# Splitting paged key loads 11 : 5 instead of 8 : 8 between SyncE's queue and GpSimd's indirect loads

## The chip, the cores and the metric

The kernel runs on one core of one Trainium2 chip. The metric is device time in microseconds (us) for one execution of the whole program, the median of several runs. Engines are named as the profile names them: PE is TensorE's matmul side and PEld its weight loads, DVE is VectorE, ACT is ScalarE, POOL is GpSimd, SP is SyncE, which here does nothing but issue transfers. An engine's queue that issues a DMA is written SPq or ACTq.

## The reference

The program is one inference step of two decoder layers on a prompt of 1024 tokens and on a sample group of 8 sequences with 4 new tokens each (32 rows), all in float32. Layer 0 mixes tokens by multi-scale pooling and retention, layer 1 by multi-head latent attention; each layer ends in a gated MLP with a width-3 causal convolution. Only layer 1's sample attention is touched by the change. Each of the 8 sequences has 8192 past tokens in a paged cache, 64 pages of 128 tokens, found through a page table:

```
ckv_past = cache_ckv[layer_idx, page_table].reshape(B, P, KV_LORA)      # 8 x 8192 x 256
kpe_past = cache_kpe[layer_idx, page_table].reshape(B, P, QK_ROPE)      # 8 x 8192 x 64
q_lat  = einsum('bqhd,chd->bqhc', q_nope, w_uk)
s_past = einsum('bqhc,bkc->bhqk', q_lat, ckv_past) + einsum('bqhr,bkr->bhqk', q_pe, kpe_past)
p      = softmax(concat([s_past, s_new]) * MLA_SCALE, masked)
o_lat  = einsum('bhqk,bkc->bqhc', p[..., :P], ckv_past) + einsum('bhqk,bkc->bqhc', p[..., P:], c_kv)
```

The prompt's attention of the same layer (8 heads, causal, 1024 x 1024) needs nothing from the cache.

## The kernel before, in words

**Stages.** The program runs layer 0 (mixer, output projection, MLP), then layer 1's projections, then `attention()`, then the output projection `om` and layer 1's MLP. Weights come in units of 128 x 1024 numbers on SP's queue and are split into a high and a low part, because each product is made of three fast matmuls.

**attention().** It holds two streams of work for PE. The prompt stream is `heads()` (keys and values of a head), `scores()` and `outs()`. The sample stream is `keys()`, `turn()`, `soft()` and `values()`. The past is read twice: as key pages, feature-major, 128 rows of 320 numbers (160 KB a page), and as value blocks of four pages, token-major, 128 rows of 4 x 257 numbers (526,336 bytes, by the shape of `vt`).

- `load_keys()` (line 1548) goes over 8 sequences, and for each over 8 key tiles `kt` of 8 pages. A tile comes from a ring of `KRAW = 4`. Line 1561 decides for each page of the tile who loads it. With `j % 4 < KSP` and `KSP = 2`, pages 0, 1, 4 and 5 go to SP and pages 2, 3, 6 and 7 to GpSimd: 256 pages each in the whole stage.
- An SP page is `page_load()` (line 1908): a `value_load` reads the page's row number from the table in SBUF into a register of SP, and a plain DMA reads 128 rows from there. The `value_load` may be issued once the DMA eight SP pages before it has been issued.
- A GpSimd page is one indirect DMA: GpSimd itself makes the list of rows from the table.
- `load_values()` (line 1569) takes a tile `vt` from a ring of `VRAW = 5` and loads each of 128 value blocks (16 for each sequence) by an indirect DMA of GpSimd. Key and value loads of GpSimd stand in one queue, in the order in which the planner came to them.
- `keys()` (line 1580) takes two key tiles at once, which is called a pair below: 16 pages. It gives 16 + 4 narrow matmuls for each pair (line 632) and gives both tiles back. There are 32 pairs.
- `values()` (line 1660) takes two `vt` tiles at once and gives 16 narrow matmuls, on the average for four `vt` tiles per pair of key tiles.

**What sets the order.** All these are generators. `Pipe.run()` picks the next step for PE when the program is written: the first in priority that is ready by a set of modelled clocks (`Clocks`, line 294 on). The instructions are then issued in that order, and each engine works through its own list in order; nothing is reordered on the chip by what really arrives. A clock stands for each of PE, DVE, ACT, POOL and SP, and one more list for the transfers:

```
issue = {"sp": 480.0, "act": 50.0, "pool": 1040.0}[eng]
...
end = self.transfer(t + issue + 700.0, size / RATE)
```

These are lines 354 and 357: a DMA takes so many ns of its issuing engine, and then `size / RATE` ns of one path, on which transfers go one after the other (`RATE = 310` bytes per ns, which is GB/s). `Engine.__getattr__` (line 398) adds 590 ns to SP's clock for each `value_load`. The sample stream has priority 5.0 and the prompt stream 5.5 to 6.0, as long as the sample stream has spent no more than `SHARE = 1.2` times the PE time of the prompt stream; so the planner gives PE sample work when its modelled data is there, and prompt work in between. The same clocks plan all other stages too, where each weight unit is one DMA of SP.

After the key pages SP's list holds the loads `uvn` and `prm`, and then the weights of `om`.

Of the kernel before, what the change touches and what calls it, by code (L numbers as in the profile page):

```python
# [43 lines left out]
CHUNKS = [(0, CH), (CH, CH), (2 * CH, CH)]  # L44
ENDS = [(0, 352), (352, 288), (640, 256), (896, 160)]
NEG = -1.0e30
KSP = 2
KRAW = 4
VRAW = 5
NST = 5  # L50
# [13 lines left out]
END2 = (2, 3)  # L64
AHEAD = 0.0
PRICE = 0.42
RATE = 310.0
SHARE = 1.2
DVEX = 0.0
HEADS = [("uqn", 0), ("uqn", 1), ("uqp", 0), ("uqp", 1), ("uqn", 2), ("uqn", 3)]  # L70
# [223 lines left out]
class Clocks:  # L294
# [52 lines left out]
    def count(self, eng, op, ins, outs):  # L347

        ext = [a for a in list(ins) + list(outs) if len(a.shape) > 1]
        n = max(int(np.prod(a.shape[1:])) for a in ext) if ext else 1  # L350
        psum = any(a.space == PSUM for a in list(ins) + list(outs))
        if "dma" in op:
            size = int(np.prod(outs[0].shape)) * 4.0
            issue = {"sp": 480.0, "act": 50.0, "pool": 1040.0}[eng]
            t = max([self.at[eng]] + [self.ready(a, eng) for a in ins] + [self.free(a) for a in outs])
            self.at[eng] = t + issue
            end = self.transfer(t + issue + 700.0, size / RATE)
            for a in outs:
                self.write(a, end, "dma")
            for a in list(ins) + list(outs):  # L360
                self.used[a.name] = max(self.used.get(a.name, 0.0), end)
            if outs[0].space != DRAM:
                self.last = max(self.last, end + self.SEEN["dma"])
            return
        small = sum(len(a.shape) == 2 and a.shape[1] == 1 for a in list(ins[1:]) + list(outs))
        if eng == "act":
            cost = n / 1.2 + (51.0 if psum else 94.0) + (93.0 if small and n > 1 else 0.0)
        elif eng == "dve":
            fast = op in ("tensor_copy", "tensor_scalar") and not psum
            cost = (66.0 + (6.0 * n if op == "reciprocal" else n / 2 if fast else n)) / 0.96  # L370
            if n > 1 and op in ("tensor_scalar", "scalar_tensor_tensor"):
                cost += 63.0 * small
        else:
            cost = {"tensor_tensor": 150.0 + 2.1 * n, "memset": 37.0 + 0.9 * n}.get(op, 120.0 + 3.3 * n)
        self.issue(eng, cost, ins, outs)
# [16 lines left out]
class Engine:  # L392
# [5 lines left out]
    def __getattr__(self, op):  # L398
        f = getattr(self._real, op)
        if op == "value_load":  # L400
            self._clocks.at["sp"] += 590.0
            return f

        def call(*args, **kw):
            r = f(*args, **kw)  # L405
            aps = [a for a in args if isinstance(a, bass.AP)]
            ins = aps[1:] + [a for k, a in kw.items() if k != "accum_out" and isinstance(a, bass.AP)]
            outs = aps[:1] + [a for k, a in kw.items() if k == "accum_out" and isinstance(a, bass.AP)]
            self._clocks.count(self._name, op, ins, outs)
            return r  # L410

        return call
# [149 lines left out]
class Kernel:  # L562
# [906 lines left out]
    def attention(self):  # L1469
# [35 lines left out]
        def load_queries():  # L1505

            for e in range(2):
                nc.sync.dma_start(qraw[64 * e:64 * e + 64], self.qpd[:, :, SEQ:])
            for e in range(2):
                nc.sync.dma_start(qpe0[64 * e:64 * e + 64], self.qpd[:, 0, :SEQ])  # L1510
            for e in range(2):
                s = slice(64 * e, 64 * e + 64)
                nc.vector.tensor_copy(qpS[s, :, e].rearrange("p b h i -> p h b i"), qraw[s].rearrange("p h (b i) -> p h b i", b=NB))
            pipe.give("p")
            pipe.fire("qps")
# [32 lines left out]
        def load_keys():  # L1548
            for b in range(NB):
                kix, o = (kix1, (b - 1) * NPG) if b else (self.kix0, 0)  # L1550
                if b == 0:
                    load_queries()
                    nc.sync.dma_start(kix1, io["ptb"][:, NPG:])
                    yield ("rd", kix1)
                    self.rows(kix1, 128.0, "part", ap.tile([128, 512], F32, tag="sev", name="rows", bufs=NEV)[:, :NB * NPG - NPG])
                for u in range(NPG // 8):
                    yield ("res", "kt", 1)
                    kt = ap.tile([128, 8, 320], F32, tag="kt", name="kt", bufs=KRAW)
                    for j in range(8):
                        n = o + u * 8 + j  # L1560
                        if j % 4 < KSP:
                            kdma.append(self.page_load(kdma, kt[:, j], kix[0:1, n:n + 1]))
                        else:
                            nc.gpsimd.indirect_dma_start(kt[:, j], None, io["kT"],
                                                         bass.IndirectOffsetOnAxis(ap=kix[:, n:n + 1], axis=0))
                    raws[b, u] = kt
                    pipe.fire(("kraw", b, u))
# [327 lines left out]
        pipe.late = XRA  # L1895
        pipe.add(prepare(), 1)
        pipe.add(load_keys(), -3)
        pipe.add(load_values(), -3)
        pipe.add(values(), sprio)
# [115 lines left out]
```

## Time and profile before

| what | value |
|---|---|
| median of 3 runs | 2901.79 us (2899.61 to 2902.35) |
| profiled execution, its own time | 2902.8 us |
| span of the profiled instructions | 2901.0 us |
| granted PE clock over the span | 0.97 |
| PE busy | 2743.6 us, 95% of the span |
| POOL busy | 850.1 us, 29% |
| DMA | 301.78 MB, mean 104 GB/s |
| key pages by SP, by GpSimd | 256, 256 |
| value blocks by GpSimd | 128 |

The page gives busy time of each engine over the whole span. The share of POOL, 29%, is an average over stages: in the second part of the page, 40 slices of 72.5 us each with the busy share in tenths, POOL stands at 7 in six slices in the middle and at 0 to 4 elsewhere. Windows are given in us from the start of the span; the stage `attention()` lies at about 1409 to 1967. In a view of windows the columns are the length, then for each engine its busy time with the number of its instructions, then PE's granted clock, the share of time in which the 16 DMA engines were busy, and the rate that they moved. In a view of waits each row says who waited for whom, with the sum in us, the number of times and the longest. A wait "<- issue" is time between two instructions in which the engine waited for nothing that the profile shows.

### The profile page before, as it was taken

What the parts mean: (1) busy time and instruction counts of PE and PEld (TensorE: products, weight loads), DVE (VectorE), ACT (ScalarE), POOL (GpSimd) and SP (SyncE); (2) the same over time, 40 slices, a digit from 0 to 9 for tenths busy, and PEclk for the clock granted to TensorE, in tenths of its full rate; (3) what the DMA queues carried; (4) which work ended last, traced back from release to release, by engine and by line L of the source; (5) the groups of instructions that cost most, each with busy time, mean ns of one, the idle gap of its engine ahead of it and who ended that gap; (6) DMA issues with size and microseconds to landing.
All of it is one profiled execution on the core that took longest, in us unless ns stands there. A gap on an engine that the chain in (4) does not pass through costs nothing.

```text
span 2901.0 us, 43639 instructions
## 1 busy us (share of the span) xinstructions
PE 2743.6 (95%) x16897; PEld 2459.3 (85%) x16897; DVE 1417.1 (49%) x2721; ACT 867.5 (30%) x1831; POOL 850.1 (29%) x884
## 2 busy tenths in 40 slices
PE   8999998999999999989888989799899999999997
PEld 6777997999999999879745555469789999999996
DVE  4444547544444444774343535355764444444455
ACT  3323435211211222243233433243431211211223
POOL 1222334010110010333577777643410110011112
PEclk9999999999999999999999999899999999999997
DMA  3111420211111111132888999874211111111101
GB/s 137 60 56 50 118 80 23 65 44 37 59 44 38 58 44 52 38 100 67 254 293 280 310 318 314 274 236 140 66 44 37 59 44 33 63 45 46 49 25 60
DMA packets 127055, 301.78 MB, mean 104 GB/s; under 512 B 20960, under 2 KB 71952, under 8 KB 126720
## 3 DMA queue, kind: packets, MB, share of 16 engines
q1 hardware_dynamic: 75648, 159.62, 16.9%
q0 software_dynamic: 32576, 113.73, 11.5%
q10 hardware_dynamic: 18624, 25.63, 3.0%
q8 instruction: 134, 2.20, 0.3%
q14 instruction: 73, 0.60, 0.1%
HBM read 283.71 MB, written 15.21 MB: 103 GB/s over the span
## 4 chain that ended last, share of the span: by engine, by line
PE 77%; DMA 6%; DVE 5%; issue 5%; POOL 4%; ACT 2%; SPq 0%; POOLq 0%; DVEq 0%; ACTq 0%
PE bank L616 70%; PE bank L632 3%; DMA kt<-in_kT,kix 3%; DMA vt<-in_vrow,vix 2%; PE sc L616 2%; POOL kt L405 2%; PE bank L638 1%; DVE x L405 1%; DVE ln_v L405 1%; DVE z L405 1%; POOL z L405 1%; DMA p<-qpd 1%; DVE wl L405 1%; DMA kt<-in_kT 1%; POOL vt L405 0%
## 5 line engine op out<-in xcount | busy, mean ns | idle before, releaser
L616 PE MATMUL bank<-x,wh 128*128 128x352 f32 x5664 | 1379.7, 326 | 18.1 <-DVE x L405 16.6
L616 PEld LDWEIGHTS bank<-x,wh 128*128 128x128 f32 x5664 | 992.8, 190 | 32.7 <-DVE x L405 21.7
L616 PE MATMUL bank<-x,wl 128*128 128x352 f32 x2832 | 915.7, 324 | 9.4 <-DVE wl L405 9.4
L616 PEld LDWEIGHTS bank<-x,wl 128*128 128x128 f32 x2832 | 537.1, 190 | 11.1 <-DVE wl L405 10.6
L405 ACT CAST wh<-wr 128x1024 fp32r<-128x1024 f32 (+1 forms) x196 | 202.7, 1041 | 669.9 <-PE bank L616 638.6
L405 DVE SCALAR_TENSOR_TENSOR z<-z,bank 128x352 f32<-128x352 f32 (+3 forms) x440 | 219.6, 511 | 325.6 <-PE bank L616 319.6
L616 PE MATMUL bank<-ah,wh 128*128 128x352 f32 (+3 forms) x1088 | 352.8, 324 | 0.0
L616 PE MATMUL bank<-ah,wl 128*128 128x352 f32 (+3 forms) x1088 | 350.3, 322 | 0.0
L616 PE MATMUL bank<-al,wh 128*128 128x352 f32 (+3 forms) x1088 | 350.2, 322 | 0.0
L405 POOL TENSOR_TENSOR wl<-wr,wh 128x1024 fp32r<-128x1024 f32 (+1 forms) x60 | 145.3, 2430 | 638.3 <-PE bank L616 391.6
L405 POOL DMA_INDIRECT kt<-in_kT,kix x256 | 252.1, 985 | 84.3 <-issue 59.9
L405 DVE TENSOR_TENSOR wl<-wr,wh 128x1024 fp32r<-128x1024 f32 (+1 forms) x138 | 176.9, 1284 | 147.9 <-ACT wh L405 143.3
L616 PE MATMUL bank<-wh,x 128*128 128x512 f32 (+3 forms) x720 | 238.7, 393 | 8.1 <-ACT wh L405 8.1
L616 PEld LDWEIGHTS bank<-ah,wh 128*128 128x128 f32 x1088 | 207.6, 191 | 1.3 <-issue 0.2
L616 PEld LDWEIGHTS bank<-al,wh 128*128 128x128 f32 x1088 | 207.4, 191 | 1.4 <-issue 0.2
L616 PEld LDWEIGHTS bank<-ah,wl 128*128 128x128 f32 x1088 | 207.5, 191 | 0.6 <-DVE wl L405 0.6
L405 POOL COPY co<-a 128x2 f32<-128x2 f32 x44 | 39.2, 892 | 553.9 <-ACT a L405 553.9
L405 DVE SCALAR_TENSOR_TENSOR y<-a,prm,y 128x352 f32<-128x352 f32 (+1 forms) x264 | 166.1, 629 | 9.8
L405 DVE TENSOR_TENSOR g<-y,bank 128x352 f32<-128x352 f32 (+2 forms) x176 | 71.5, 427 | 202.2 <-PE bank L616 201.1
L405 DVE TENSOR_SCALAR y<-a,prm 128x352 f32<-128x352 f32 x132 | 77.0, 583 | 183.6 <-ACT a L405 178.1
L616 PEld LDWEIGHTS bank<-wh,x 128*128 128x128 f32 (+1 forms) x720 | 127.6, 181 | 32.5 <-ACT wh L405 8.1
L405 POOL DMA_INDIRECT vt<-in_vrow,vix x128 | 125.8, 983 | 72.8 <-PE bank L632 28.1
(234 smaller groups left out, 3184.4 us busy)
## 6 DMA issues: line engine op xcount, KB each, us to landing
wr<-in_w_up SPq DMA_DIRECT2D x88, 512.0 KB
kt<-in_kT SPq DMA_DIRECT2D x256, 160.0 KB
wr<-in_w_dn SPq DMA_DIRECT2D x44, 512.0 KB
wr<-in_w_h SPq DMA_DIRECT2D x16, 512.0 KB
wr<-in_w_oe SPq DMA_DIRECT2D x16, 512.0 KB
wr<-in_w_om SPq DMA_DIRECT2D x16, 512.0 KB
z<-in_xT SPq DMA_DIRECT2D x12, 352.0 KB
z<-in_xT ACTq DMA_DIRECT2D x3, 1408.0 KB
```

What stands on the lines that cost most here:

```text
L405: r = f(*args, **kw)
L616: self.nc.tensor.matmul(out, lhsT, rhs, start=start, stop=stop)
L632: self.nc.tensor.matmul(out[32 * g:32 * g + m], lhsT, rhs, start=start, stop=stop, tile_position=(0, 32 * g))
L638: self.nc.tensor.transpose(out, in_, self.ident[:in_.shape[0], :in_.shape[0]])
```

## The change

It does three things.

1. `KSP` becomes 11 and the rule on line 1561 counts pages over two tiles: page number `n16 = u * 8 + j` goes to SP when `n16 * 11 % 16 < 11`. Of each 16 pages, 0, 2, 3, 5, 6, 8, 9, 11, 12, 14 and 15 go to SP, five in the first tile of a pair and six in the second; 1, 4, 7, 10 and 13 go to GpSimd. In all SP loads 352 pages and GpSimd 160.
2. The clocks' prices: a DMA takes 530 ns of SP instead of 480 and 1250 ns of GpSimd instead of 1040, and a `value_load` 570 ns instead of 590.
3. The clocks' path: `RATE` 380 instead of 310. This and the prices enter the planner alone; they change no instruction, but the order in which instructions of each engine are issued.

```
-KSP = 2
+KSP = 11
...
-RATE = 310.0
+RATE = 380.0
...
-            issue = {"sp": 480.0, "act": 50.0, "pool": 1040.0}[eng]
+            issue = {"sp": 530.0, "act": 50.0, "pool": 1250.0}[eng]
...
-            self._clocks.at["sp"] += 590.0
+            self._clocks.at["sp"] += 570.0
...
-                        if j % 4 < KSP:
+                        if (u * 8 + j) * KSP % 16 < KSP:
                             kdma.append(self.page_load(kdma, kt[:, j], kix[0:1, n:n + 1]))
                         else:
                             nc.gpsimd.indirect_dma_start(kt[:, j], None, io["kT"],
```

## The prediction

> **What bounds the kernel now.** First the page's slices, to find the stage; in each row a digit is the busy share of a slice in tenths.
>
> ```profile
> PE   8999998999999999989888989799899999999997
> POOL 1222334010110010333577777643410110011112
> DMA  3111420211111111132888999874211111111101
> ```
>
> POOL and DMA are high only in slices 20 to 26. The view of windows, cut at that stage's borders, measures it:
>
> ```profile
> core 0: us, PE busy (x) PEld busy (x) DVE busy (x) ACT busy (x) POOL busy (x), PEclk, DMA share, GB/s
> 0.00:1409.00 1409.00, 1357.63 (x7990) 1272.43 (x7991) 705.20 (x1326) 413.09 (x845) 305.27 (x344) 0.99 0.20 65
> 1600.00:1860.00 260.00, 231.04 (x1638) 138.43 (x1636) 111.22 (x282) 94.09 (x247) 194.68 (x197) 0.93 0.92 307
> 1409.00:1876.00 467.00, 403.41 (x2742) 238.77 (x2740) 188.58 (x483) 162.11 (x419) 345.54 (x350) 0.91 0.91 302
> 1876.00:1967.00 91.00, 85.42 (x661) 62.24 (x660) 51.25 (x139) 39.96 (x114) 41.54 (x41) 0.96 0.63 209
> 1967.00:2901.00 934.00, 897.11 (x5507) 885.82 (x5507) 472.02 (x774) 252.35 (x454) 157.71 (x149) 0.97 0.17 54
> ```
>
> The stage is two parts: 467 us up to the last key matmul, and 91 us of leftover values and prompt work. PE is busy 403.41 + 85.42 = 488.8 of 558 us and idle for 69.2, 63.6 of them in the first part. PE's work in the stage is fixed, so the change can only move these 69.2 us (and the clock, 0.91 in the first part against 0.99 before the stage). The view of PE's waits in this window says what they are:
>
> ```profile
> PE bank L632 <- DMA vt<-in_vrow,vix: 36.8, 19, 8.9
> PE bank L632 <- ACT pn L405: 7.6, 2, 6.7
> PE bank L638 <- ACT p L405: 7.1, 1, 7.1
> PE bank L616 <- ACT th L405: 6.1, 6, 2.5
> PE bank L632 <- DMA kt<-in_kT,kix: 3.9, 2, 2.9
> ```
>
> 40.7 us wait for loaded data, 36.8 for values and 3.9 for keys, and all of it for transfers that GpSimd issued. The other rows are the softmax's own turnaround, which the change does not touch. Now the three things that could pace the loads, in the settled middle, 1600 to 1860. The groups of POOL (busy, mean ns, idle before) and the DMA queues:
>
> ```profile
> L405 POOL DMA_INDIRECT kt<-in_kT,kix x130 | 129.1, 993 | 44.2 <-issue 29.9 <-PE bank L632 5.9 <-DMA kt<-in_kT,kix 4.3
> L405 POOL DMA_INDIRECT vt<-in_vrow,vix x66 | 64.9, 983 | 21.2 <-issue 9.0 <-PE bank L632 3.0 <-DMA kt<-in_kT,kix 2.7
> ```
>
> ```profile
> GB/s 198 380 290 353 389 179 319 333 311 371 217 357 262 373 347 271 384 216 322 320 309 368 222 377 226 319 383 345 373 286 383 222 330 357 174 268 280 300 314 237
> q0 software_dynamic: 15537, 55.23, 62.0%
> q1 hardware_dynamic: 18432, 20.98, 24.8%
> q10 hardware_dynamic: 928, 3.15, 5.2%
> ```
>
> 130 key pages are 130/8 = 16.25 pairs of tiles, so a pair takes 260/16.25 = 16.0 us. GpSimd: 129.1 + 44.2 + 64.9 + 21.2 = 259.4 of 260 us are its 196 loads with the gaps between them, 1.32 us each; a pair needs 8 + 4 of them, 15.9 us. It is full. DMA engines: 0.92 of 16.0, 14.7 us a pair. PE: 231.04/16.25 = 14.2 us. SP's own pace, from its timeline, first eight pages each behind its value_load, then its waits in the same window:
>
> ```profile
> 1583.16 8.71 SPq L405 DMA_DIRECT2D kt<-in_kT  x8
> ```
>
> ```profile
> SPq L405 <- PE bank L632: 61.6, 10, 8.6
> SPq L405 <- PE bank L616: 36.5, 7, 12.8
> SPq L405 <- PE bank L638: 9.7, 3, 5.8
> ```
>
> That is 1.09 us a page, 8.7 us a pair; 61.6 + 36.5 + 9.7 = 107.8 us, 6.6 us a pair, it stands and waits for PE to give back key tiles. So GpSimd (15.9) ends last, with the DMA engines (14.7) and PE (14.2 and its turnaround) close behind.
>
> **The change part by part.** *The move of 96 pages.* A pair now asks 5 + 4 loads of GpSimd, 9 x 1.32 = 11.9 us, and 11 x 1.09 = 12.0 us of SP. Both fall below today's 16.0, so neither queue is the pace any more in the middle. SP's added 3 x 1.09 = 3.3 us a pair go into the 6.6 us in which it waits now; if that cover were gone, they would cost up to 32 x 3.3 = 105 us, but this would take an SP that PE never kept waiting. At the start values are not yet used, as the view of tiles shows (duration, first and last start):
>
> ```profile
> L632 PE MATMUL bank<-kt,qlT x512: 589/592/1063, 1419.0 to 1874.1; 128*32 128x512 f32 x171
> L632 PE MATMUL bank<-vt,sT x1024: 380/380/637, 1474.0 to 1944.4; 128*32 128x257 f32 x171
> ```
>
> Up to 1474 SP's 12.0 us a pair stand against GpSimd's 8 x 1.32 = 10.6, so these first six or so pairs come 1.4 us later each; prompt work covers that, and it is 8 us if it does not. SP's list behind the key pages (`uvn`, `prm`, the weights of `om`) is issued no later, since those weights wait for the end of the stage. The bytes stay; by the rows of the queues a page by either queue loads the same 16 engines (55.23 MB in 62.0% is 343 GB/s at full share, 20.98 MB in 24.8% is 325), so 15.7 MB moved from one to the other change 96 x 163,840/325 − 96 x 163,840/343 = 2.5 us of DMA time, out of 467.
>
> What is late next is the DMA engines: with GpSimd out of the way the pace can go from 16.0 to 14.7 at full share, and PE's 14.2 plus the turnaround not touched (69.2 − 40.7 = 28.5 us, 0.9 a pair) is 15.1. So with an order like today's the pace becomes about 15.1, PE's own, and the waits for data would go: at most 40.7 us.
>
> The Trainium skill, page "DMA: Bandwidth & Descriptors", section "Issuing engines are not separate DMA queues", speaks against the change: DMAs of all engines run on the same sixteen, and a second issuer saves only issue time, which it calls usually small beside the transfer. This trace agrees on the first half (62.0 + 24.8 + 5.2 = 92% on one set of engines) and not on the second, since issuing fills 259.4 of 260 us here. By the Trainium skill alone the change would give nothing, which is a rival below.
>
> *The clocks.* Prices near the measured ones let the planner put GpSimd's loads where they will be: 1250 against the measured 1.32 us, where 1040 let it plan each pair 12 x 0.28 = 3.4 us too early. That is why values come late. *The path.* A pair moves 16 x 163,840 + 4 x 526,336 = 4.73 MB. At 310 the planner gives it 15.3 us, within 0.7 of the real 16.0: today's order and the loads march in step. At 380 it gives 12.4. The slices show 371 to 389 GB/s in nine of forty, but the mean is 307 at a share of 0.92, 334 at full share; so real pairs will not come in 12.4 us, and the planner puts less prompt work between them. PE then waits for data, and the prompt work that it did not do stands behind the last values. No row shows an order made at 380. Bounds: nothing, if the planner's order is set by PE's work rather than by its path (14.2 of its 16 us are work); and 14.7 − 12.4 = 2.3 us for each of 32 pairs, 74 us of waits in place of 40.7, a loss of 33. I take half the gain of the first part for it: of the 36.8 us that PE waits for values 18.4 go and as much stays, as waits for keys and values that are still on the way. This lies between a gain of 40.7 and a loss of 33, nearer to the gain, because the queue that ends every pair today is relieved by a quarter, which is certain.
>
> The Trainium skill, on the same page "DMA: Bandwidth & Descriptors", section "Specifications", gives about 358 GB/s as the limit of HBM for one core. An estimate from it: 4.73 MB at 358 take 13.2 us, so 380 would be out of reach for the mean; slices of 389 in the trace show it passed for some us, and no row shows it passed for longer.
>
> *Other stages.* There each weight unit is one DMA; cheaper path time may move some steps of the order. PE is busy 1357.63 of 1409 and 897.11 of 934 us with DMA shares of 0.20 and 0.17, so loads are long there before their use: 0, between −3 and +3 us.
>
> **Sum.** 2902.8 (its span of 2901.0 and 1.8 around it) − 18.4 = 2884.4. The median of the runs shown is 1.0 below the profiled execution: 2883.4, rounded 2883. For the likeliest case alone I allow 2870 to 2895, some twelve us to either side.
>
> **Rivals.**
>
> *The waits go altogether.* For it: GpSimd has all of the waits for data, and PE's clock in the stage is 0.91 to 0.93 against 0.99 outside, so fewer stops also give faster matmuls. Against: 14.7 us of DMA a pair leave little below 15.1. 40.7 us less, and up to 10 by the clock (a third of 403.41 x (0.99 − 0.91)): 2851 to 2861. Chance 0.17.
>
> *The transfers are the pace anyway.* The share of 0.92 is as full as these loads get; the queues only wait in another place, and waits for `kt` take the place of those for `vt`. For it: 14.7 of 16.0. Against: SP and GpSimd together could then ask for 4.73 MB in 12.0 us, and slices reach 389 GB/s. The order's shift and small gains cancel: 2896 to 2907. Chance 0.18; it holds also the case that the change does its part and other stages give it back.
>
> *The order runs ahead of the data* (slower). The planner's 12.4 us a pair against a real pace of more; every pair PE stops for the difference, in the middle of sample work, and prompt work lies behind the last values with no loads left to cover. It decides when the real pace stays more than 12.4 + 40.7/32 = 13.7 us a pair and the order follows the path fully. At 14.7 the loss is 33 us; where half of the order follows, about 17: 2919. For it: the mean rate, 334 at full share. Against: 14.2 us of each pair are PE's work, and the SP clock, 11 x (530 + 570) = 12.1 us a pair, holds the planner back as well. Chance 0.25, over 2908 to 2935.
>
> **How the numbers follow.** The forecast has 0.40; the larger gain 0.17; no change 0.18; slower 0.25. What can be told from no change in this kernel is about 0.2%, 5.8 us. A little of the forecast's and the ordering case's inner ends lies within that: faster 0.57, same 0.18, slower 0.25. Cases of both signs hold the chance, so the range that holds 8 in 10 reaches from 2850, the end of the larger gain, to 2922, in the middle of the slower case; the likeliest case's own is 2870 to 2895.
>
> **What the profile of the changed kernel would show.** Right: in the middle of the stage POOL's loads with their gaps fill some 75% in place of 259.4 of 260; SP's waits for PE shrink; the DMA share is 0.95 or more and a pair takes about 15 us; the waits of PE for `vt` halve. Wrong: POOL still back to back; or PE waiting for `kt` and `vt` more than 40.7 us with the last key matmul sooner than at 1876 and more than 91 us behind it, which is the order running ahead; or the DMA share at 0.92 again with a pair in 16 us.

## The result and the profile after

The changed kernel takes 2919.22 us, the median of 5 runs (2915.31 to 2925.62), against 2901.79 of the kernel before on the same chip: a ratio of 1.0058, 95% interval 1.0044 to 1.0073. It is slower by 17.4 us, where the prediction had it faster by 19. The profiled execution took 2925.6 us (span 2923.8), 22.8 more than the profiled one of before.

The view of windows of the changed kernel, cut at its own borders: last key matmul at 1853, first matmul of `om` at 1990.

```profile
0.00:1409.00 1409.00, 1359.57 (x7988) 1275.03 (x7989) 706.07 (x1324) 413.91 (x847) 304.74 (x343) 0.99 0.20 65
...
1600.00:1800.00 200.00, 179.00 (x1279) 102.50 (x1278) 86.58 (x218) 69.79 (x184) 122.53 (x126) 0.97 1.00 347
...
1409.00:1853.00 444.00, 389.86 (x2658) 229.08 (x2656) 185.63 (x474) 154.66 (x405) 249.15 (x253) 0.94 0.94 316
1853.00:1990.00 137.00, 117.12 (x747) 80.76 (x748) 59.44 (x150) 47.32 (x130) 41.22 (x41) 0.84 0.43 147
1990.00:2923.00 933.00, 896.09 (x5507) 884.65 (x5506) 470.09 (x773) 252.18 (x453) 159.87 (x150) 0.97 0.17 54
```

What comes before the stage and after it is unchanged: 1409 us, and 933 in place of 934. The part behind the last key matmul is called the tail from here; it is 46 us longer (137 for 91). The first part of the stage is 23 us shorter (444 for 467). 46 − 23 = 23 us is the whole difference. Of the 23 us of the first part only 9.5 are idle time that PE lost (54.1 us for 63.6). In the other 13.5 PE is less busy (389.86 us for 403.41), and these are no gain: the matmuls that are missing there, 2658 for 2742, stand in the tail, 747 for 661.

The loads did come sooner. In 1600 to 1800 the DMA engines are full, 1.00 at 347 GB/s. The queues and issues of that window:

```profile
q0 software_dynamic: 11305, 40.47, 55.9%
q1 hardware_dynamic: 22798, 25.95, 39.0%
...
kt<-in_kT SPq DMA_DIRECT2D x156, 160.0 KB
...
kt<-in_kT,kix POOLq DMA_INDIRECT x73
```

156 + 73 = 229 pages are 14.3 pairs, 14.0 us each; the kernel before has 104 + 102 = 206 pages in the same window, 15.5 us a pair. GpSimd now stands and waits, and SP hardly does. The waits of POOL in 1409 to 1853, then those of SP:

```profile
POOL kt L405 <- DMA kt<-in_kT: 53.4, 27, 8.0
POOL kt L405 <- PE bank L632: 43.5, 13, 7.2
POOL vt L405 <- PE bank L632: 35.7, 22, 6.6
```

```profile
SPq L405 <- DMA kt<-in_kT: 22.3, 21, 2.7
SPq L405 <- PE bank L632: 3.7, 5, 2.7
```

PE's waits in the whole stage:

```profile
PE bank L616 <- ACT th L405: 18.0, 8, 5.7
PE bank L632 <- DMA vt<-in_vrow,vix: 12.1, 11, 1.9
PE bank L632 <- DMA kt<-in_kT,kix: 10.5, 2, 5.5
PE bank L632 <- DMA kt<-in_kT: 7.8, 5, 3.7
PE bank L638 <- DVE mxa L405: 6.6, 4, 4.8
```

The waits for values fell from 36.8 to 12.1, those for keys rose from 3.9 to 18.3; together 30.4 for 40.7. Those for `ACT th`, a copy that ScalarE makes for the prompt stream, rose from 6.1 to 18.0, of which 16.8 lie in the first part.

The tail is where the time went. PE's groups there, first of the kernel before (1876 to 1967), then of the changed one (1853 to 1990):

```profile
L616 PE MATMUL bank<-th,vv 128*128 128x256 f32 (+1 forms) x80 | 21.8, 407 | 0.8 <-ACT th L405 0.8
L632 PE MATMUL bank<-vt,sT 128*32 128x257 f32 x288 | 19.8, 387 | 1.7 <-DMA vt<-in_vrow,vix 1.6
L638 PE MATMUL bank<-ident,p 128*128 128x128 f32 x72 | 13.1, 295 | 0.8 <-DVE amx L405 0.8
...
L616 PE MATMUL bank<-kvT,uh 128*128 128x512 f32 x8 | 2.6, 402 | 0.0
```

```profile
L632 PE MATMUL bank<-vt,sT 128*32 128x257 f32 x288 | 26.2, 454 | 5.8 <-DMA vt<-in_vrow,vix 5.8
L616 PE MATMUL bank<-th,vv 128*128 128x256 f32 (+1 forms) x92 | 25.7, 411 | 1.3 <-ACT th L405 1.2
L638 PE MATMUL bank<-ident,p 128*128 128x128 f32 x79 | 16.0, 322 | 3.8 <-DVE p L405 3.8
...
L616 PE MATMUL bank<-kvT,uh 128*128 128x512 f32 x16 | 7.7, 557 | 0.0
L616 PE MATMUL bank<-wv,kvT 128*128 128x256 f32 x48 | 6.4, 285 | 0.0
...
L616 PE MATMUL bank<-ol,cst 128*128 128x1 f32 x6 | 1.2, 273 | 3.0 <-DVE ol L405 3.0
...
L638 PE MATMUL bank<-ident,mxa 128*32 128x128 f32 x2 | 0.7, 372 | 5.0 <-DVE mxa L405 5.0
```

Twelve more `th,vv` matmuls, and the keys and values of a whole head pair (`kvT,uh`, `wv,kvT`; before, the keys of one head) stand behind the last key now: prompt work that the kernel before had done while the pages came. The 288 value matmuls are the same in number and take 26.2 us for 19.8, and the granted clock in the tail is 0.84 for 0.96. The timeline of the changed kernel has eight of them in a row in 0.64 us at 1885, where the clock is 1.00, and in 1.08 us at 1892, where it is 0.50. PE's busy time in the tail is up by 117.12 − 85.42 = 31.7 us and its idle time by 19.9 − 5.6 = 14.3.

### The profile page after: what moved, and what is told of

The parts are those of the page before. It is cut to its first block, busy times and chain, and to the rows that moved or that the text cites. A ratio compares the mean times of both kernels' runs of the same rounds, so it can differ in the third digit from the quotient of the medians.

```text
span 2923.8 us, 44128 instructions
## 1 busy us (share of the span) xinstructions
PE 2762.6 (94%) x16897; PEld 2469.5 (84%) x16897; DVE 1421.2 (49%) x2720; ACT 868.1 (30%) x1833; POOL 755.0 (26%) x787
## 4 chain that ended last, share of the span: by engine, by line
PE 79%; DVE 6%; DMA 5%; issue 5%; ACT 2%; POOL 2%; SPq 1%; ACTq 0%; DVEq 0%; POOLq 0%
PE bank L616 71%; PE bank L632 4%; DMA kt<-in_kT 3%; PE sc L616 2%; PE bank L638 2%; DVE ln_v L405 1%; DVE x L405 1%; DVE z L405 1%; DMA kt<-in_kT,kix 1%; DMA p<-qpd 1%; SPq L405 1%; DMA vt<-in_vrow,vix 1%; SPq L1914 1%; POOL z L405 1%; DVE wl L405 1%
## 5 line engine op out<-in xcount | busy, mean ns | idle before, releaser
L405 POOL DMA_INDIRECT kt<-in_kT,kix x160 | 158.8, 992 | 133.3 <-DMA kt<-in_kT 53.4
```

## The experiments

One thing has to be known first: the experiments ran on four chips on which the kernel before takes 3039 to 3053 us, not 2902. One of the four was used twice and gave 3041.98 and 3053.45. Whether the chip itself makes the difference to 2902, or something else that differed between the runs, is not shown. The profile of the kernel before on one of them (`f2_before`) shows the difference in the stage `attention()` alone:

```profile
0.00:1409.00 1409.00, 1357.24 (x7985) 1272.49 (x7986) 706.06 (x1326) 412.50 (x845) 304.10 (x344) 0.99 0.21 65
```

```profile
1409.00:2008.00 599.00, 463.89 (x2746) 270.80 (x2744) 190.76 (x481) 161.58 (x419) 341.62 (x350) 0.84 0.73 232
2008.00:2105.00 97.00, 88.48 (x665) 64.50 (x661) 52.55 (x140) 39.99 (x114) 42.32 (x42) 0.93 0.66 219
```

Up to the stage the two traces agree (1357.24 and 1357.63 us busy of 1409). In it the DMA engines are less busy, 0.73 for 0.91, and PE stops where the profile shows no releaser:

```profile
PE bank L616 <- issue: 33.7, 22, 8.5
PE bank L632 <- issue: 21.0, 35, 1.3
```

With two smaller rows that is 67.7 us, against one row of 0.5 us in the kernel before on the chip of the result. In all the stage is 138 us longer (696 for 558): PE is idle for 143.6 us in place of 69.2 and busy for 552.4 in place of 488.8, at a clock of 0.84 for 0.91 in the first part. What sets the pace differs too. The waits of POOL for key tiles and value tiles to come back from PE, in the first part on the chip of the result and then here:

```profile
POOL kt L405 <- PE bank L632: 8.5, 9, 3.3
POOL vt L405 <- PE bank L632: 7.3, 8, 3.6
```

```profile
POOL kt L405 <- PE bank L632: 60.3, 20, 11.7
POOL vt L405 <- PE bank L632: 57.6, 15, 12.4
```

GpSimd's key loads are as long as there (983 ns for 985 in the mean), but GpSimd stands and waits for PE, and PE waits for loaded data for 9.2 us only, in place of 40.7. So on these chips GpSimd's queue is not what holds the kernel before up, and a gain of the split there is not the gain that the prediction reckoned with. So ratios on these chips stand for these chips, and tails and orders can be compared with the result's only with that in mind. Three theories were tried. A: the order made with the new clocks runs ahead of the loads and leaves prompt work in the tail. B: the split itself costs, by SP's queue. C: GpSimd's loads cost more on some chips, so that the split's worth depends on the chip. The last column counts PE's matmuls from the end of the last key matmul to the first of `om`.

| kernel | split | RATE | prices | before, us | time, us | ratio, 95% interval | tail, us | matmuls in it |
|---|---|---|---|---|---|---|---|---|
| f2_before | 8 : 8 | 310 | old | 3039.36 | 3041.11 (one run) | | 96 | 660 |
| e2_clocks_only | 8 : 8 | 380 | new | 3041.98 | 3029.72 | 0.9959 (0.9946 to 0.9973) | 95 | 666 |
| f4_clocks_only | 8 : 8 | 380 | new | 3039.36 | 3029.96 | 0.997 (0.9954 to 0.9986) | 95 | 666 |
| e1_split_only | 11 : 5 | 310 | old | 3041.98 | 2942.05 | 0.9679 (0.9659 to 0.9698) | 87 | 602 |
| f3_split_only | 11 : 5 | 310 | old | 3039.36 | 2940.88 | 0.968 (0.9666 to 0.9695) | 84 | 602 |
| h1_split_only | 11 : 5 | 310 | old | 3043.34 | 2945.82 | 0.9681 (0.9666 to 0.9695) | 89 | 602 |
| i1_split_only | 11 : 5 | 310 | old | 3040.80 | 2941.32 | 0.967 (0.9653 to 0.9687) | 85 | 602 |
| j2_split_only | 11 : 5 | 310 | old | 3053.45 | 2952.42 | 0.9672 (0.9654 to 0.9691) | 82 | 602 |
| e3_after_r310 | 11 : 5 | 310 | new | 3041.98 | 2960.99 | 0.9736 (0.972 to 0.9753) | 86 | 602 |
| h3_split_rate260 | 11 : 5 | 260 | old | 3043.34 | 2986.44 | 0.982 (0.9804 to 0.9835) | 76 | 366 |
| j1_split_rate340 | 11 : 5 | 340 | old | 3053.45 | 2963.21 | 0.9709 (0.9692 to 0.9725) | 93 | 660 |
| h2_split_rate380 | 11 : 5 | 380 | old | 3043.34 | 2977.68 | 0.9788 (0.9774 to 0.9802) | 108 | 726 |
| f1_after | 11 : 5 | 380 | new | 3039.36 | 2991.66 | 0.9837 (0.9823 to 0.9852) | 134 | 745 |
| e4_after_share06 (SHARE 0.6) | 11 : 5 | 380 | new | 3041.98 | 2985.87 | 0.9819 (0.9806 to 0.9833) | 46 | 228 |
| i2_split_13 | 13 : 3 | 310 | old | 3040.80 | 2951.74 | 0.9707 (0.9693 to 0.9722) | 79 | 522 |
| h4_all_sp | 16 : 0 | 310 | old | 3043.34 | 3009.41 | 0.9889 (0.9874 to 0.9904) | 54 | 272 |

The count is a matter of the program, since PE works through its list in order. On the chip of the result it is 660 for the kernel before and 745 for the changed one, as here. The time that this work takes can differ by chip; that it stands in the tail does not.

**The split alone.**

```
-RATE = 380.0
+RATE = 310.0
...
-            issue = {"sp": 530.0, "act": 50.0, "pool": 1250.0}[eng]
+            issue = {"sp": 480.0, "act": 50.0, "pool": 1040.0}[eng]
...
-            self._clocks.at["sp"] += 570.0
+            self._clocks.at["sp"] += 590.0
```

> The 11 : 5 split with the planner's old clocks (RATE 310, prices 480, 1040 and 590). Theory A, the order made at 380 runs ahead of the data and leaves prompt work behind the last values: without it the split shows its own worth, 2882 to 2902, the last key matmul at 1850 to 1865 and about 91 us of stage behind it. Theory B, the split itself costs (SP is now back to back and keys come late by its queue): 2915 to 2925, as with the whole change.

2942.05 us, 0.9679: a gain of 3.2% where the whole change, on another such chip, gains 1.6%. Theory B falls on these chips; on the chip of the result the split alone was not run. The absolute numbers of the expectation were for the chip of the result and do not apply.

**The clocks alone**: the kernel before with the new clocks.

```
-RATE = 310.0
+RATE = 380.0
...
-            issue = {"sp": 480.0, "act": 50.0, "pool": 1040.0}[eng]
+            issue = {"sp": 530.0, "act": 50.0, "pool": 1250.0}[eng]
...
-            self._clocks.at["sp"] += 590.0
+            self._clocks.at["sp"] += 570.0
```

> The old 8 : 8 split with the new clocks (RATE 380, prices 530, 1250 and 570). Theory A: GpSimd stays the pace at 16 us a pair and the order asks for more, so PE's waits for data exceed 40.7 us and the leftover behind the last key matmul exceeds 110 us: 2915 to 2940. Theory B: 2897 to 2907, as before.

0.9959, with a tail of 95 us for 96. Theory A as I stated it was wrong here: with the old split the new clocks leave no prompt work behind. Its reason can be read from the planner's own prices: GpSimd's 12 loads a pair at 1250 ns are 15.0 us, so the old split is planned at 15.0 us a pair whatever the path says. Only with the 9 loads of the new split (11.3 us) and SP's 12.1 is the path's 12.4 the last. That is argued from the prices; that the tail stays is measured.

**The whole change with RATE 310.**

```
-RATE = 380.0
+RATE = 310.0
```

> The whole change with RATE back at 310 and the new issue prices. Theory A: RATE is what moved the order, so 2882 to 2902. Theory B: 2915 to 2925. A third possibility, that the issue prices move the order and not RATE: 2915 to 2925 here while the split with all old clocks is at 2882 to 2902.

2960.99 us, between the split alone (2942.05 on the same chip) and the whole change (2991.66 on another), with a tail of 86 us and 602 matmuls in it, as with the split alone. So the new issue prices cost 19 us with this split even at 310, not in the tail but mostly before it (last key at 1931 for 1919), and the longer tail comes with RATE.

**SHARE 0.6.** The kernel differs from the changed one in one line, RATE stays 380:

```
-SHARE = 1.2
+SHARE = 0.6
```

> The whole change with SHARE 0.6 in place of 1.2: the planner lets the sample stream take at most 0.6 of the prompt stream's PE time before prompt work goes first, so prompt work is spread over the stage whatever RATE says. Theory A: the leftover behind the last key matmul falls from 137 us to about 90 and the time to 2880 to 2905. Theory B: the keys come no sooner, 2915 to 2930.

The tail falls to 46 us, as an order with more prompt work early must have it, but the last key comes at 2000 in place of 1923, and the time is 2985.87. Both A and B missed. That a fixed share holds key tiles back as long as prompt work goes first would explain the late key; it is argued, not measured.

**Both kernels and both halves on one chip.** The changed kernel, the kernel before and the two halves, side by side.

> The whole change once more, beside the kernel before on the chip of this call. The chip of the first four experiments ran the kernel before in 3042 us, the chip of the result in 2902. Theory A (the order runs ahead of loads that cannot come faster): slower than before by 0.3 to 0.8% where GpSimd's loads run at 1.3 us each without stops; on a chip like that of the first four it lies between the split alone (0.968) and the clocks alone (0.996), at 0.97 to 0.985. Theory C (GpSimd's queue costs more on some chips, so the split's worth depends on the chip): faster by 2 to 3% there, slower on a chip like that of the result.

> The kernel before, for its trace on the chip of this call. If it takes about 3040 us, theory C expects waits for GpSimd's loads or gaps between them that the trace of 2902.8 us does not have; if about 2902 us, the trace as it was.

> The split with the old clocks again, on the chip of this call. Theory A: faster than the whole change by 15 to 35 us and, where before takes 2902, 2880 to 2902. Theory B (the split itself costs): there 2915 to 2925, as the whole change.

> The old split with the new clocks again, on the chip of this call. Theory A: where before takes 2902, 2910 to 2940; where it takes 3042, 0.99 to 1.00 of it, as it was. Theory B: within 0.2% of before.

The split alone gains 98 us, the clocks alone 9, both together 48: the clocks cost 51 us when the split is there, more than the 15 to 35 expected. The ratio of the whole change, 0.9837, lies in theory A's range for such a chip, and its gain of 1.6% short of the 2 to 3% of theory C. The windows of the split alone and of the whole change say where:

```profile
1409.00:1922.00 513.00, 427.08 (x2794) 254.61 (x2793) 201.40 (x515) 168.29 (x444) 249.50 (x254) 0.92 0.85 273
1922.00:2005.00 83.00, 75.12 (x602) 51.84 (x602) 40.09 (x107) 31.41 (x87) 39.84 (x41) 0.98 0.71 237
```

```profile
1409.00:1923.00 514.00, 419.56 (x2656) 242.19 (x2654) 185.88 (x474) 153.50 (x404) 248.14 (x253) 0.88 0.85 272
1923.00:2057.00 134.00, 113.68 (x748) 78.89 (x746) 58.71 (x149) 47.28 (x129) 41.25 (x41) 0.86 0.45 153
```

The last key comes at the same time, 1922 and 1923, with the same DMA share (0.85) and nearly the same rate. But the first has given PE 2794 matmuls by then and the second 2656; the 138 to 146 missing ones stand in the tail, 748 for 602, which takes 134 us for 83. This is theory A on this chip: an order planned for faster data makes the data no faster and leaves work behind it. PE's waits for loaded data do not show it: they come to 17.2 us in the split alone and to 12.8 in the whole change. The whole change's tail is the same as on the chip of the result, 134 and 137 us, with 748 and 747 matmuls.

**RATE by itself**: the split alone with RATE 380, 260 and 340 and the old prices.

```
-RATE = 310.0
+RATE = 380.0
```

> The split with the old issue prices and RATE 380, so that RATE stands alone. If RATE moves the prompt work behind the last key matmul: the stage behind it takes 110 to 140 us and the time is 20 to 50 us over the split alone. If it is the issue prices that do it: within 8 us of the split alone.

> The split with the old issue prices and RATE 260, the other way: more prompt work between the pairs, less behind the last. Theory A: where before takes 2902 the real pace is near 14 us a pair and 260 plans 18.2, so key tiles are held by PE and the last key comes later; 2885 to 2905, slower than at 310. Where before takes 3040 the real pace is 15.5 to 16 and the order may fit as well as at 310: within 12 us of the split alone, to either side.

> The split with the old issue prices and RATE 340, between 310 and 380. If the tail grows with RATE step by step (89 us at 310, 108 at 380): about 97 us, and 10 to 25 us over the split alone, 2950 to 2970 where before takes 3040. If the optimum lies above 310: at or below the split alone, 2930 to 2945. Where before takes 2902, with loads that march faster, 340 could fit as well as 310: 2870 to 2895.

2977.68 at 380 and 2986.44 at 260, beside 2945.82 for the split alone; on another chip 2963.21 at 340, beside 2952.42: on these chips 310 is the best of the four. The tail goes 76, 82 to 89, 93, 108 us from 260 to 380, and the matmuls in it 366, 602, 660, 726. At 260 the expectation missed, since the loss over the split alone is 41 us and not at most 12, and it is on the other side:

```profile
1409.00:1975.00 566.00, 479.86 (x3050) 302.86 (x3049) 220.04 (x582) 194.50 (x519) 251.81 (x255) 0.91 0.78 247
1975.00:2051.00 76.00, 52.02 (x368) 21.68 (x367) 18.38 (x39) 6.53 (x15) 41.56 (x42) 0.63 0.77 267
```

PE does 3050 matmuls before the last key, holds key tiles meanwhile (1975 for about 1920), and the tail has only values left, PE idle for 24 of 76 us. With the new prices the tail at 380 is 134 and not 108. It holds 745 matmuls in place of 726, at a clock of 0.86 for 0.97 and with 20.3 us of idle time for 9.7. The path rule above does not explain this difference, and it stays open.

**Other splits.** All pages by SP, and thirteen of sixteen, with the old clocks:

```
-KSP = 11
+KSP = 16
```

```
-KSP = 11
+KSP = 13
```

> All 16 of 16 pages by SP, old clocks: GpSimd issues values alone, 4 x 1.32 = 5.3 us a pair, and SP 16 x 1.09 = 17.4 us. SP is then the pace: the last key matmul not before 1409 + 32 x 17.4 = 1966, with a tail of 85 to 95, so the time is 2985 to 3010 on any chip. If GpSimd's queue alone were what costs, it would be at or below the split alone.

> Thirteen of sixteen pages by SP, old clocks: GpSimd 3 + 4 loads a pair, 9.2 us, SP 13 x 1.09 = 14.2 us. Theory C (on chips with 3040 each key load of GpSimd costs stops of PE that no releaser explains: 65 us at 256, 17 to 27 at 160, 2 at none): stops of 8 to 18 us at 96. The pace is then SP's, 14.2 us a pair, where eleven gave 15.9 in the real order: 2925 to 2950 there. If the stops have nothing to do with GpSimd's loads, 17 to 27 us of them stay. Where before takes 2902: 2875 to 2900.

All by SP: 3009.41, within the range, but by two errors that cancel: the last key comes at 2018 where 1966 was the least by SP's pace, and the tail is 54 us where 85 to 95 were expected. SP waits for others for 4.2 us only, so its own pace was 1.19 us a page and not 1.09. PE waits for loaded data for 65 of its 117 us of idle time. Thirteen: 2951.74, 0.9707, just above the range and near the split of eleven (0.967 on the same chip). PE's stops without a releaser go with GpSimd's key loads: 67.7 to 92.4 us at 256 loads, 21.1 to 49.2 at 160, 7.4 at 96 (two of its three rows below; 8 to 18 were expected) and 12.6 at none, where 10.2 are of one row (the expectations' 2 us counted longer stops alone).

```profile
PE bank L616 <- issue: 3.0, 4, 1.8
PE sc L616 <- issue: 2.9, 2, 2.5
```

That supports theory C in part: on these chips some of the split's 3.2% goes with the end of stops that the chip of the result does not have. The loads themselves are not longer, as said above; 96 and none were run once each, and the run with none is not the one with the fewest stops. What stops PE there stays open.

**Where before takes 2902.** The split alone was run three more times, and on each of these chips the kernel before took 3040 us or more.

> The split with the old clocks, once more, in the hope of a chip on which the kernel before takes about 2902 us. Theory A: there the last key matmul comes at 1850 to 1860 as in the whole change, since the loads are the same, and the stage behind it takes 83 to 90 us in place of 137: 2870 to 2885, a ratio of 0.989 to 0.994. Theory B (the split itself costs there): 2910 to 2925. Where before takes 3040: 0.968 again.

> The split with the old clocks beside the kernel before. If the chip runs the kernel before in about 2902 us: theory A 2870 to 2885 (last key matmul at 1850 to 1860, 83 to 90 us of stage behind it), theory B 2910 to 2925. If it runs it in about 3040: 0.968, as three times.

> The split with the old clocks, a last time for a chip on which the kernel before takes about 2902 us: there theory A 2870 to 2885, theory B 2910 to 2925. Elsewhere 0.967 of about 3040, 2935 to 2950.

The three results are in the table above. The split alone has thus five ratios of 0.967 to 0.968 on these chips and none on the chip of the result.

## Why the prediction was wrong

- **What bounds the stage: right on the chip of the result.** GpSimd was the pace. With 9 loads a pair it waits (53.4 + 43.5 + 35.7 us in three rows), and the DMA engines are next, at 1.00.
- **The new pace: right in kind, too cautious in size.** I had 14.7 us a pair at full share and 15.1 by PE's own pace; it is 14.0 in 1600 to 1800, where the full rate is 347 GB/s and not 334. PE's pace gave way: with less prompt work between the pairs PE is busy for 179.00/14.3 = 12.5 us a pair, not 14.2, so it was no floor.
- **SP's cover: gone.** SP waited 6.6 us a pair for PE; now its rows for PE sum to some 8 us in 444. Key tiles are waited for more, 18.3 for 3.9 us, which the prediction set at nothing; whether the split or the order makes these waits is not shown on this chip.
- **The step that failed: "I take half the gain of the first part for it".** It put the cost of RATE 380 into PE's waits for data and set 18.4 us of them as the net gain. Those waits did fall, by 10.3. The cost did not show there: it is work displaced into the tail, 745 matmuls for 660, which no wait for data measures, and the tail grew by 46 us. I had named it in a rival ("prompt work lies behind the last values with no loads left to cover"), had priced it by waits again, and gave it 0.25. That the rival's price, 2919, is the measured time is luck: it stands for some 17 us more of waits for data, and these became fewer.
- **The signs named for being right came, and the time was wrong.** SP's waits for PE shrank, the DMA share reached 1.00, a pair took 14.0 us and the waits for values fell to a third. Of the sign for the order running ahead two parts came, the last key at 1853 and 137 us behind it, and one did not, 30.4 us of waits where more than 40.7 were named. The work behind the last key was the part to look at.
- **What the tail costs.** 46 us: some 14 of waits and 32 of busy time. The waits are for values (5.8 us for 1.6) and for short steps of VectorE between matmuls (`mxa` 5.0, `p` 3.8 and `ol` 3.0, against 0.8 for `amx` before); that there is too little other work in the tail to fill them is argued. The extra matmuls at the durations of the tail before (clock 0.96) are about 17 of the busy time: 12 x 0.27 for `th,vv`, 8 x 0.32 for `kvT,uh`, 48 x 0.13 for `wv,kvT` and some 5 us of smaller groups. This is an estimate, since the groups overlap. The other 15 go with the clock, 0.84 in the tail; busy time times clock gives about the same, 117.12 x 0.84 − 85.42 x 0.96 = 16 us of work at full clock. The unchanged 288 value matmuls alone lost 6.4 us.
- **"PE's work in the stage is fixed, so the change can only move these 69.2 us": half wrong.** PE's idle time rose by 4.8 us only (69.2 to 74.0). PE's busy time rose by 18.2 (488.8 to 507.0), on the same work. I had noted the clock as something to gain and did not price its loss. It is not all of it: the first part won some of the clock (0.94 for 0.91) that the tail lost (0.84 for 0.96). The clock records of the two traces have PE busy at half clock for 63.5 us of the stage before and 84.0 after; half of the difference, some 10 us, is an estimate of the clock's share of the 18.2. What makes up the other 8 stays open.
- **Which part of the change it was.** That the split gains and the clocks take back half of it is shown on chips where before takes 3040 us, with the tail as the measured place. On the chip of the result only the two ends are measured. That the clocks put the work into the tail holds there too, since the counts are the program's: 602 matmuls with the split alone, 745 with the clocks. What the split alone would take there does not follow. If its first part were 444 us again and its tail 84, as the first part and the tail were on one other chip, it would be 2902.8 − 558 + 528 = 2873, an estimate. It has not been measured, so that the split itself costs something there is not ruled out.

The new split with the old clocks beats the kernel before on all four chips where it ran, and both kernels on the one where all three did: 2940.88 against 2991.66 and 3039.36 us.

## What to carry to other kernels

When a planner fixes an in-order engine's list, its modelled rate decides how much independent work is put under the loads; after a load is made faster, look at both ends, because an order that asks for data sooner than it comes leaves that cover for the end, where there are few loads left to cover. Price such a change by the work that stands behind the last load, not by the engine's waits for data, which can fall while the time rises. Measure a change of queues apart from the retuning that comes with it: here one gained 3.2% and the two together 1.6%, or lost 0.6%, by the chip.

## What the runs showed of the hardware that was not expected

- The same kernel takes 2902 us on one chip and 3039 to 3053 on four, all of the difference in the stage with dense loads, with the DMA engines less busy there (0.73 for 0.91), PE busy for 63.6 us more at a lower clock (0.84 for 0.91) and stopping 67.7 us for no releaser in the profile. What makes the difference is not shown.
- On the four chips those stops are fewer with fewer of GpSimd's indirect key loads, but do not end with them: 67.7 to 92.4 us at 256, 21.1 to 49.2 at 160, 7.4 at 96, 12.6 at none.
- The sixteen DMA engines held 347 GB/s over 200 us at a share of 1.00, where the kernel before's full share came to 334.
- A low granted clock can outlast the stop that it follows. In the tail of the changed kernel PE stands for 4.2 us in 1880 to 1890; in the next 20 us it is busy for 19.7, at half clock. That the stop makes the low clock is not shown: in 1970 to 1980 PE stands for 3.3 us, and the clock is 0.96.

```profile
1880.00:1890.00 10.00, 5.84 (x64) 1.98 (x63) 3.84 (x5) 0.58 (x1) 6.47 (x7) 0.85 0.87 287
1890.00:1900.00 10.00, 9.67 (x39) 3.98 (x40) 4.64 (x8) 2.63 (x6) 4.82 (x5) 0.50 0.70 249
1900.00:1910.00 10.00, 10.00 (x50) 6.38 (x49) 3.12 (x13) 2.08 (x6) 3.21 (x4) 0.50 0.55 171
...
1970.00:1980.00 10.00, 6.68 (x37) 5.34 (x35) 7.07 (x14) 5.04 (x14) 3.71 (x3) 0.96 0.29 106
```
